# Experts of the second layer: a fixed TensorE order, gate and up side by side, mix in row groups

## The chip, the cores and the metric

The kernel runs on one core of one Trainium2 chip. The metric is the device time of one execution in microseconds (us), the median of several runs. The core has five engines with queues of their own: TensorE (PE; its weight loads are shown as PEld), VectorE (DVE), ScalarE (ACT), GpSimd (POOL) and SyncE (SP), which issues most of the DMAs.

## What is computed

A model of two layers runs over 256 tokens and 256 context tokens, 1024 wide. Each layer is a mixer (a recurrent scan, a neighbourhood attention and a sliding-window attention) and a mixture of 16 experts, of which each token takes two. In the second layer only the 256 tokens are left. The change touches that layer's experts:

```python
def moe(h, w_router, router_bias, w_gate, w_up, w_down):
    ...
    y = jnp.zeros_like(h)
    for e in range(N_EXPERTS):
        he = jax.nn.silu(h @ w_gate[e]) * (h @ w_up[e])
        y = y + gates[:, e:e + 1] * (he @ w_down[e])
    return y

# in reference(), last layer
f = moe(h2.reshape(-1, d), w_router, router_bias, w_gate[l], w_up[l], w_down[l]).reshape(x.shape)
x = layer_norm(alpha * x + g2 * f, ln2_g[l], ln2_b[l])
```

`gates` is zero but for two experts of a token. An expert's weights are three matrices, 1024 x 512 twice and 512 x 1024, 6 MiB in float32.

## The kernel before

**Capacities.** The kernel sorts the experts by how many tokens chose them and gives the place in that order a fixed capacity. In the second layer these are 64 for places 0 to 2, 128 for place 3, 64 for places 4 to 10 and 32 for places 11 to 15. A path for tokens that don't fit (`rerun`) follows under a condition and isn't taken here.

**One expert in the second layer** (`experts1`), with the tiles' names as the profile shows them:

1. The six pieces of its weights, 1 MiB each (`wload`), come in order over SP's queue into a ring of 16 pieces of SBUF. A piece's load waits until the matmuls that read the piece's last content have ended.
2. `hgather`: 48 small bfloat16 matmuls with a one-hot matrix (`oh`) put the expert's tokens, transposed, into PSUM (tile `hgt`); ScalarE copies them to region C.
3. `half`, for gate and then for up: `contract` multiplies the tokens (stationary) with the weights (moving, 512 columns) in float32, eight steps of k; each is two MATMUL instructions in the trace. A stationary matrix of 64 columns fills half of the array's columns, so two steps of k stand side by side, in two column groups (four for capacity 32). Their sums lie in different partitions of one PSUM bank (tile `gu`).
4. `whole` adds these row groups up: one ScalarE copy and one VectorE addition for two groups, one copy and three additions for four. `glu` applies SiLU on ScalarE and multiplies gate by up, on POOL for all but the last expert.
5. `htrans`: four transposes (tile `hT`), a ScalarE copy to region A.
6. `down`: `contract` again, into two banks (tile `dn`), one for each half of the 1024 columns, with two or four row groups each.
7. `weigh`: ScalarE scales both banks by the gate value into a rounded float32r part, and VectorE writes the remainder; VectorE also makes the matrix (`st`) that sends rows back to tokens. `slot` supplies the token numbers and gate values for that, by two small matmuls.
8. `mix`: eight float32r matmuls, 128 rows by 512 columns, add the expert's rows into four PSUM banks that stay for the whole layer (tile `acc`): this also adds the row groups of `down` up.

**Order.** The instructions are written in a software pipeline: the gate half of expert i, the transposes of i - 1, the slot of i + 1, the mix of i - 2, the up half of i, the gather of i + 1, down of i - 1. A scheduler may move an instruction ahead of others on its engine where no dependence forbids it.

**Staging region.** Elsewhere in the kernel float32 weights are split into two float32r parts in region S (16 K elements a partition, K = 256), which `split` fills in turn. In the second layer's experts S holds the scaled rows of `weigh`.

**After the experts** come the residual, a layer norm and the output.

Of the kernel before, what the change touches and what calls it, by code (L numbers as in the profile page):

```python
# [67 lines left out]
REGIONS = {"A": 16 * K, "B": 8 * K, "C": 8 * K, "S": 16 * K}  # L68
# [103 lines left out]

class _Builder:
    def __init__(self, tc, ap, out, dbg=None, caps=CAPS):
        self.tc, self.nc, self.ap, self.out, self.dbg, self.caps = tc, tc.nc, ap, out, dbg or {}, caps
# [5 lines left out]
    def run(self):  # L181
        tc = self.tc
        with ExitStack() as ctx:
# [19 lines left out]
            with tc.If(cnt > 0):  # L203
                self.general, self.native, self.map = True, False, BANKS
                self.lastw = self.hold = self.lastg = None
# [55 lines left out]
    def split(self, raw, dst=None):  # L261
        if dst:
            hi, lo = dst
        else:
            n = raw.shape[1]
            u = n // 256
            m = sum(t.shape[1] for t in self.sring) // 512
            if self.nsp % m + u > m:
                self.nsp += m - self.nsp % m
            o = (self.nsp % m) * 512  # L270
            self.nsp += u
            r = self.sring[0]
            if o >= r.shape[1]:
                o, r = o - r.shape[1], self.sring[1]
# [239 lines left out]
    def mixer(self, l):  # L514
        self.tokens_in()
        self.ring_of("S")
# [694 lines left out]
    def finish(self, l, T, rows):  # L1211
# [108 lines left out]
        self.ring_of("S")  # L1320
# [255 lines left out]
    def hsplit(self, i, cap, put):  # L1576
        nc = self.nc
        if self.single(cap):
            if not self.native:
                self.ring_of("S")  # L1580
# [23 lines left out]
    def contract(self, pbs, h, w):  # L1604
# [3 lines left out]
        if len(h) == 1:  # L1608
            m = P // cap
            for g in range(0, nk, m):  # L1610
                for j, pb in enumerate(pbs):
                    for i in range(m):
                        o = ((g + i) * n + j) * 512
                        t = slice(i * cap, (i + 1) * cap)
                        nc.tensor.matmul(pb[t], h[0][:, g + i], w[o // PIECE][:, o % PIECE:o % PIECE + 512],  # L1615
# [10 lines left out]
        return [pb[:cap] for pb in pbs]  # L1626

# [25 lines left out]
    def htrans(self, i, a, cap, pb=None):  # L1653
# [13 lines left out]
        for k in range(4):  # L1667
            nc.tensor.transpose(pb[:, k * cap:(k + 1) * cap], av[:, k, :], self.ident[:cap, :cap])  # L1668
# [26 lines left out]
    def wload(self, l, e, names):  # L1695
        out = []
        for n in names:
            for i in range(2):
                t = self.ring[self.nr % len(self.ring)]
                self.nr += 1  # L1700
                eng = self.nc.sync
                if e < self.fix:
                    src = self.ap[n][l * NE + e]
                else:
                    src = self.ap[n][bass.ds(self.expert(l, e - self.fix), 1)].rearrange("o p c -> p (o c)")
                self.lastw = eng.dma_start(t, src[:, i * PIECE:(i + 1) * PIECE])
                out.append(t)
        return out
# [7 lines left out]
    def start(self, l):  # L1716
# [12 lines left out]
        self.ring_of("S") if l else self.ring_of("C", "S")  # L1729
# [140 lines left out]
    def hgather(self, i, cap):  # L1870
# [3 lines left out]
        def put(o, k):  # L1874
            for tb, v in enumerate(oh):
                for j in range(3):
                    nc.tensor.matmul(o, self.hp[tb][j][:, k, :], v[:, :cap], start=tb + j == 0, stop=3 * tb + j == n - 1)  # L1877
# [3 lines left out]
    def slot(self, i, pi):  # L1881
        nc, oh = self.nc, self.oh
        M = oh[0].shape[1]
        for tb, v in enumerate(oh):
            nc.tensor.matmul(pi[:M, :5], v, self.meta[:, tb, i, :], start=tb == 0, stop=tb == 1)
# [5 lines left out]
    def weigh(self, i, pys, T):  # L1891
        nc = self.nc
        M = pys[0].shape[0]
        o = i % 2 * 2 * D
        y = [self.region("S")[:M, o + j * D:o + (j + 1) * D] for j in range(2)]
# [9 lines left out]
        def mix():  # L1905
            for tb in range(2):
                for n in range(2):
                    for j in range(2):
                        nc.tensor.matmul(self.pf[tb][n], oT[tb], y[j][:, n * 512:(n + 1) * 512],  # L1909
# [4 lines left out]
    def experts1(self, T):  # L1914
# [10 lines left out]
        load = lambda i, *names: self.wload(l, i, ["w_" + n for n in names])  # L1925
        gu = {0: load(0, "gate", "up")}
# [5 lines left out]
        a, h4, dn, ps = {}, {}, {}, {}  # L1932
        mix = None

        def down(i):
            return self.weigh(i, self.down(h4[i], dn[i]), T)

        def turn(i):
            pb = self.bank("hT")
            h4[i] = self.htrans(i, a[i], caps[i], pb)  # L1940
            return pb[:, 256:] if caps[i] <= 64 else self.bank("sl")

        self.slot(0, self.bank("sl"))
        for i in range(NE):
# [162 lines left out]
```

## Time and profile before

| | us |
|---|---|
| median of 3 runs | 1202.23 (1201.42 to 1206.09) |
| profiled execution | 1204.09 |
| its span | 1202.3 |
| busy in the span: PE / DVE / ACT / POOL | 1087.1 / 781.9 / 555.7 / 147.4 |
| granted TensorE clock, mean | 0.955 |
| read from HBM | 316.27 MB |

The span is the time from the first to the last instruction that the profiler recorded. A line of the kernel that is a helper's stands for all its callers, so tiles' names say more than lines. PEclk, or the granted clock, is the share of 2.4 GHz that TensorE got; it has two levels, 2.4 and 1.2 GHz, and a value between them is a mean over a stretch. "<-" behind an idle time names the engine and tile that ended it.

### The profile page before, as it was taken

Reading aid. Unit: us, or ns where it says so; the run is one execution under the profiler, and the core shown is the slowest. Engines: PE = TensorE matmul, PEld = TensorE weight load, DVE = VectorE, ACT = ScalarE, POOL = GpSimd, SP = SyncE. Lnnn points to the kernel's source line nnn. Section 1 sums busy time; section 2 is a strip of 40 time slices with the busy share of each in tenths; the row PEclk is TensorE's granted clock in tenths of the full one; section 3 lists DMA queues with packets and bytes.
Section 4 is the critical chain, followed back from the end, with each engine's and each line's share of the span. In section 5 each row is a group of like instructions: output and inputs, shape, how many; then the busy total and the mean of one; then the engine's idle time right before and its main releaser. Section 6 shows DMA issues by size and latency. Waiting matters only on the chain.

```text
span 1202.3 us, 18417 instructions
## 1 busy us (share of the span) xinstructions
PE 1087.1 (90%) x6813; PEld 700.1 (58%) x6813; DVE 781.9 (65%) x1742; ACT 555.7 (46%) x910; POOL 147.4 (12%) x151
## 2 busy tenths in 40 slices
PE   5999999999995999999999689999995899999872
PEld 3766766755684777676443587677664444444331
DVE  3466779757789998888324874787867622333545
ACT  2364335446643876787433644524465222222232
POOL 0000111100001243444210000010000000000000
PEclk9999999999996999999999899999896999999996
DMA  9756665634467999899999723565085699999951
GB/s 378 277 218 255 239 251 213 244 123 145 163 226 245 334 359 335 310 388 393 372 410 414 291 86 136 183 227 191 15 323 206 275 390 342 394 422 421 420 224 39
DMA packets 55044, 326.88 MB, mean 272 GB/s; under 512 B 9435, under 2 KB 9691, under 8 KB 19616
## 3 DMA queue, kind: packets, MB, share of 16 engines
q1 hardware_dynamic: 43920, 275.34, 59.5%
q0 software_dynamic: 9152, 50.10, 11.1%
q8 instruction: 56, 0.92, 0.3%
q10 hardware_dynamic: 1872, 0.16, 0.1%
q14 instruction: 44, 0.36, 0.1%
HBM read 316.27 MB, written 13.09 MB: 274 GB/s over the span
## 4 chain that ended last, share of the span: by engine, by line
PE 71%; DVE 15%; DMA 6%; ACT 5%; issue 2%; POOL 1%; SPq 0%; POOLq 0%; ACTq 0%; DVEq 0%
PE gu L1615 12%; PE proj L414 11%; PE gu L1624 7%; PE dn L1615 6%; PE op L709 4%; PE dn L1624 4%; PE first L414 3%; DMA G<-in_w_ada_dram 3%; PE acc L1909 2%; PE ada L393 2%; PE hgt L1877 2%; PE pt L1122 2%; PE S L1099 2%; PE py L1129 2%; PE hT L1668 1%
## 5 line engine op out<-in xcount | busy, mean ns | idle before, releaser
L276 ACT CAST S<-G 128x1024 fp32r<-128x1024 f32 (+2 forms) x162 | 156.9, 975 | 164.0 <-PE proj L414 108.2
L286 DVE TENSOR_TENSOR S<-G,S 128x1024 fp32r<-128x1024 f32 (+2 forms) x144 | 166.8, 1168 | 79.2 <-ACT S L276 76.9
L414 PE MATMUL proj<-A,S 128*128 128x512 f32 (+1 forms) x672 | 184.2, 355 | 2.8 <-ACT S L276 1.4
L1615 PE MATMUL gu<-G,C 128*64 128x512 f32 (+2 forms) x672 | 145.4, 602 | 1.4 <-ACT C L1597 1.4
L414 PEld LDWEIGHTS proj<-A,S 128*128 128x128 f32 x672 | 118.5, 192 | 28.9 <-issue 8.4
L1615 PEld LDWEIGHTS gu<-G,C 128*64 128x64 f32 (+2 forms) x672 | 43.4, 133 | 81.0 <-issue 76.1
L1624 PE MATMUL gu<-S,A 128*128 128x512 f32 (+3 forms) x300 | 76.6, 397 | 3.5 <-POOL S L284 2.2
L1624 PEld LDWEIGHTS gu<-S,A 128*128 128x128 f32 (+3 forms) x300 | 52.0, 177 | 20.3 <-POOL S L284 3.1
L414 PE MATMUL proj<-B,S 128*128 128x512 f32 (+1 forms) x168 | 60.2, 359 | 1.2 <-DVE B L1286 1.2
L1637 DVE TENSOR_TENSOR vt<-vt,gu 64x512 f32<-64x512 f32 (+1 forms) x31 | 21.1, 680 | 61.5 <-ACT vt L1634 61.2
L709 PE MATMUL op<-S,A 128*128 128x512 f32 x176 | 60.6, 407 | 0.0
L414 PE MATMUL proj<-C,S 128*128 128x512 f32 (+1 forms) x168 | 58.2, 348 | 0.0
L1647 POOL TENSOR_TENSOR tmp<-tmp,vt 64x512 f32<-64x512 f32 (+1 forms) x14 | 17.9, 1277 | 300.5 <-DVE vt L1637 286.5
L386 POOL DMA_DIRECT2D G<-in_w_ada_dram x40 | 22.3, 558 | 256.9 <-PE ada L393 172.2
L1637 DVE TENSOR_TENSOR tmp<-tmp,gu 64x512 f32<-64x512 f32 (+1 forms) x31 | 21.1, 680 | 50.1 <-ACT tmp L1634 49.7
L1615 PE MATMUL dn<-G,A 128*64 128x512 f32 (+2 forms) x240 | 53.3, 630 | 0.0
L1624 PE MATMUL dn<-S,B 128*128 128x512 f32 (+3 forms) x192 | 52.2, 406 | 0.4
L1624 PE MATMUL gu<-C,A 128*128 128x512 f32 (+3 forms) x180 | 48.5, 400 | 1.8 <-DVE C L286 1.8
L1567 POOL DMA_INDIRECT G<-h2d,idx x16 | 22.3, 1392 | 218.5 <-DVE oh L1551 140.5
L276 ACT CAST C<-G 128x1024 fp32r<-128x1024 f32 x38 | 39.8, 1047 | 12.3 <-PE gu L1624 7.7
L1901 DVE SCALAR_TENSOR_TENSOR S<-dn,slot,S 128x512 fp32r<-128x512 f32 x32 | 23.6, 749 | 31.9 <-ACT S L1900 30.6
L1111 ACT ACTIVATE G<-G,nm 128x512 f32<-128x512 f32 x48 | 34.5, 719 | 20.6 <-DVE nm L1109 10.2
(434 smaller groups left out, 2169.8 us busy)
## 6 DMA issues: line engine op xcount, KB each, us to landing
G<-in_w_gate_dram SPq DMA_DIRECT2D x62, 1024.0 KB, 7.9
G<-in_w_up_dram SPq DMA_DIRECT2D x62, 1024.0 KB, 8.0
G<-in_w_down_dram SPq DMA_DIRECT2D x62, 1024.0 KB, 9.5
G<-in_w_ada_dram POOLq DMA_DIRECT2D x40, 1024.0 KB, 6.7
G<-in_w_in_dram SPq DMA_DIRECT2D x22, 1024.0 KB, 8.7
G<-in_w_out_dram SPq DMA_DIRECT2D x12, 1024.0 KB, 6.3
G<-in_w_ada_dram SPq DMA_DIRECT2D x8, 1024.0 KB, 15.7
G<-vd SPq DMA_DIRECT2D x12, 512.0 KB, 4.6
```

What stands on the lines that cost most here:

```text
L276: self.lasts = [self.nc.scalar.copy(hi, raw)]
L286: self.lasts.append(sub(lo, raw, v))
L393: nc.tensor.matmul(pb[g:g + 32, i * 256:(i + 1) * 256], self.sT[:, kb, :], w[i][:, kb * 256:(kb + 1) * 256], start=kb < 4, stop=kb >= 4, t ...
L414: self.nc.tensor.matmul(pb[:, t], a[:, c], m, start=first and n == 0 and i == 0, stop=last and n == len(kbs) - 1 and i == 2)
L709: nc.tensor.matmul(pbs[tb][h], a, w[j][h], start=n == 0 and i == 0, stop=n == KB - 1 and i == 2)
L1099: nc.tensor.matmul(pb, qT[r, qb * P:(qb + 1) * P], kT[r, :], start=True, stop=True)
L1111: nc.scalar.activation(Pt, Pt, AF.Exp, scale=-1.0, bias=m, accum_out=ls[:, i:i + 1])
L1122: nc.tensor.transpose(pt[:, k * P:(k + 1) * P], Ps[i][:, k * P:(k + 1) * P], self.ident)
L1129: nc.tensor.matmul(py[r, :NX], V(hh, k), PT[hh][:, k, :], start=k == 0, stop=k == 3)
L1615: nc.tensor.matmul(pb[t], h[0][:, g + i], w[o // PIECE][:, o % PIECE:o % PIECE + 512], start=g == 0, stop=g + m == nk, tile_position=(0, i ...
L1624: nc.tensor.matmul(pbs[j][:cap], h[a][:, k], ws[b][:, c], start=k == 0 and q == 0, stop=k == nk - 1 and q == 2)
L1637: self.nc.vector.tensor_add(out, out, pb[i * cap:(i + 1) * cap])
```

## The change

- Gate and up of an expert of capacity 64 or 32 are computed together: half of the array's column groups hold gate, half up, for the same k (`tiles`). With capacity 64 there is nothing left to add up; with 32 there are two row groups for each, one copy and one addition (`fused`). SiLU reads PSUM, and the product is VectorE's. The pieces are loaded in the order gate, up, gate, up.
- `down` of these experts puts the two halves of the 1024 columns side by side in one bank (`outs`), so `weigh` scales one bank, and `mix` uses 64-row matmuls: the upper and lower half of the rows, each in a row group of the array and each into a bank of its own.
- TensorE's instructions of this stage are chained: each must follow the one written before it (`_Chained`). They are written in a new order: gather of i + 1, mix of i - 1, slot of i + 1, transposes of i, first gate-and-up half of i + 1, down of i, second half of i + 1.
- Region S becomes two tiles, S and T, of 8 K each. T is the 17th piece of the ring in the second layer's experts.
- The expert of capacity 128 keeps `contract`, in the new order.

```diff
-REGIONS = {"A": 16 * K, "B": 8 * K, "C": 8 * K, "S": 16 * K}
+REGIONS = {"A": 16 * K, "B": 8 * K, "C": 8 * K, "S": 8 * K, "T": 8 * K}
...
+class _Chained:
...
+    def _then(self, i):
+        if self.last is not None:
+            self.b.behind(i, self.last)
+        self.last = i
+        return i
...
+    def twin(self, cap):
+        return self.native and 2 * cap <= P
+
+    def tiles(self, pb, h, src, ks):
+        nk, cap = h[0].shape[1:]
+        q = P // cap // 2
+        for g in range(ks.start, ks.stop, q):
+            for j in range(2):
+                for i in range(q):
+                    o = (j * q + i) * cap
+                    self.pe.matmul(pb[o:o + cap], h[0][:, g + i], src(g + i, j), start=g == 0, stop=g + q == nk,
+                                   tile_position=(0, o))
+        return pb
+
+    def outs(self, h, w):
+        part = lambda k, n: w[k // 2][:, (2 * (k % 2) + n) * 512:(2 * (k % 2) + n + 1) * 512]
+        return self.tiles(self.bank("dn"), h, part, range(4))
+
+    def fused(self, pb, cap):
+        nc = self.nc
+        a = self.st("tmp", 512)[:cap]
+        g, u = (pb[j * P // 2:j * P // 2 + cap] for j in range(2))
+        if 4 * cap <= P:
+            for j, v in enumerate((a, self.st("vt", 512)[:cap])):
+                o = j * P // 2
+                nc.scalar.copy(v, pb[o + cap:o + 2 * cap])
+                nc.vector.tensor_add(v, v, pb[o:o + cap])
+                g, u = (v, u) if j == 0 else (g, v)
+        nc.scalar.activation(a, g, AF.Silu)
+        nc.vector.tensor_mul(a, a, u)
+        return a
...
         def mix():
+            if len(pys) == 1:
+                for tb in range(2):
+                    for j in range(2):
+                        for n in range(2):
+                            p = slice(n * P // 2, (n + 1) * P // 2)
+                            self.pe.matmul(self.pf[tb][n], oT[tb][p], y[j][p], start=i + j == 0,
+                                           stop=i == NE - 1 and j == 1, tile_position=(n * P // 2, 0))
+                return
...
+        self.ring.insert(-1, self.region("T", F32))
+        names = [("w_gate", 0), ("w_up", 0), ("w_gate", 1), ("w_up", 1)]
...
+        self.pe = _Chained(self)
...
         for i in range(NE):
-            ps[i] = [self.half(h[i], gu[i][0:2])]
...
-            pb = turn(i - 1) if i else self.bank("sl")
...
+            a = self.fused(ps[i], caps[i]) if self.twin(caps[i]) else self.glu(ps[i], caps[i])
             if i < N:
-                self.slot(i + 1, pb)
+                gu[i + 1] = [gload(i + 1, 0)]
+            dn[i] = self.wload(l, i, ["w_down"])
+            if i < N:
+                gu[i + 1].append(gload(i + 1, 1))
+                h[i + 1] = self.hgather(i + 1, caps[i + 1])
             if mix:
                 mix()
-            ps[i].append(self.half(h[i], gu[i][2:4]))
-            a[i] = self.glu(ps[i], caps[i], eng=nc.gpsimd if i < N else None)
...
+                self.slot(i + 1, self.bank("sl"))
...
+            h4 = self.htrans(i, a, caps[i])
             if i < N:
-                h[i + 1] = self.hgather(i + 1, caps[i + 1])
-            if i:
-                mix = down(i - 1)
...
+                gate(i + 1, 0)
+            if i == N:
+                break
+            mix = self.weigh(i, [self.outs(h4, dn[i])] if self.twin(caps[i]) else self.down(h4, dn[i]), T)
+            gate(i + 1, 1)
```

TensorE's queue before, in the middle of the experts of capacity 64, from one gather to the next (a MATMUL row of gu, dn, acc or hT counts matmuls of the program; "oh" is the one-hot matrix, "st" the matrix of the mix):

```order
L1615 MATMUL dn<-G,A 64x512 x8
L1615 MATMUL gu<-G,C 64x512 x8
L1668 MATMUL hT<-con,tmp 128x64 x4
L1909 MATMUL acc<-S,st_8397 128x512 x4
L1885 LDWEIGHTS oh
L1885 MATMUL hT<-meta,oh 128x5
...
L1909 MATMUL acc<-S,st_8398 128x512 x4
L1615 MATMUL gu<-G,C 64x512 x8
```

The same place now, again from one gather to the next:

```order
L184 MATMUL acc<-S,st_8405 128x512 x4
L184 MATMUL acc<-S,st_8406 128x512 x4
L184 LDWEIGHTS oh
L184 MATMUL sl<-meta,oh 128x5
...
L187 MATMUL hT<-con,tmp 128x64 x4
L184 MATMUL gu<-G,C 64x512 x8
L184 MATMUL dn<-G,A 64x512 x8
L184 MATMUL gu<-G,C 64x512 x8
```

The mix and the transposes moved ahead of both gate-and-up halves, directly behind the gather, and down of the same expert moved between the halves of the next one; a step that stood between two halves of one expert is now between two experts.

ScalarE's queue before, over one expert of capacity 32 (tmp is the gate's row sum and then SiLU, vt the row sum of up, S the scaled rows, C the gathered tokens, A the transposed ones):

```order
L1597 COPY A<-hT 128x128
L1634 COPY tmp<-gu 32x512
L1643 ACTIVATE tmp<-tmp 32x512
L1597 COPY C<-hgt 128x256
L1634 COPY vt<-gu 32x512
L1900 ACTIVATE S<-dn,slot 128x512 x2
```

ScalarE's queue now, over one expert of capacity 32:

```order
L1670 COPY tmp<-gu 32x512
L1614 COPY C<-hgt 128x256
L1670 COPY vt<-gu 32x512
L1673 ACTIVATE tmp<-tmp 32x512
L1614 COPY A<-hT 128x128
L1950 ACTIVATE S<-dn,slot 128x512
```

Both copies of row sums now stand ahead of SiLU, with the copy of the gathered tokens between them, and one scaled copy is left of two. VectorE's additions on gu go from six to two for such an expert and from two to none for one of capacity 64.

## Rows read from the trace of the kernel before

**Rows 1.** Stretches: busy us (x instructions) of each engine, PEclk, DMA share, GB/s.
```profile
1030.00:1040.00 10.00, 10.00 (x50) 4.23 (x48) 3.94 (x10) 3.15 (x6) 0.70 (x1) 1.00 0.98 365
1043.00:1108.00 65.00, 65.00 (x511) 29.05 (x510) 23.49 (x48) 18.45 (x32) 6.35 (x5) 1.00 1.01 422
1108.00:1183.00 75.00, 60.96 (x536) 25.99 (x528) 37.00 (x75) 21.59 (x40) 5.09 (x4) 0.93 0.68 281
1170.00:1180.00 10.00, 7.41 (x28) 2.94 (x28) 4.72 (x8) 1.67 (x4) 0.00 (x0) 0.66 0.01 2
```
**Rows 2.** Chain of waits, one expert of capacity 64: start us, us, what.
```profile
1042.95 1.51 PE hgt L1877 x48
...
1051.47 0.62 PE hT L1668 x4
1052.10 1.13 PE acc L1909 x4
...
1053.27 1.03 PE acc L1909 x4
1054.31 3.58 PE gu L1615 x16
1057.89 1.51 PE hgt L1877 x48
```
**Rows 3.** Timeline of PE in the second mixer: start, us, engine, line, tile, shape.
```profile
853.22 0.71 PE L981 MATMUL lev<-G 64*128 64x128 f32 x8
...
854.75 1.04 PE L1122 MATMUL pt<-con,G 128*128 128x128 f32 x8
```
**Rows 4.** Chain of waits, first gate of expert 1 and of expert 11.
```profile
947.70 3.65 PE gu L1615 x16
...
1107.60 1.00 PE gu L1615 x8
```
**Rows 5.** Chain of waits, the experts of capacity 32.
```profile
1139.73 0.59 ACT tmp L1634
...
1142.51 1.37 PE hgt L1877 x48
...
1151.11 1.90 PE gu L1615 x16
...
1155.86 1.37 PE hgt L1877 x48
```
**Rows 6.** Groups by form, 934 to 1184 us: line, engine, tile, shape, count, busy, mean ns.
```profile
L1901 DVE SCALAR_TENSOR_TENSOR S<-dn,slot,S 128x512 fp32r<-128x512 f32 x32 | 23.6, 749 | 31.9 <-ACT S L1900 30.6
L1900 ACT ACTIVATE S<-dn,slot 128x512 fp32r<-128x512 f32 x32 | 21.5, 687 | 38.3 <-PE dn L1615 38.2
...
L1637 DVE TENSOR_TENSOR tmp<-tmp,gu 32x512 f32<-32x512 f32 x15 | 10.2, 682 | 8.4 <-ACT tmp L1634 8.0
...
L1903 DVE TENSOR_SCALAR st<-Sd,slot 128x128 fp32r<-128x128 f32 x32 | 9.0, 283 | 17.2 <-PE acc L1909 9.3 <-PE hT L1885 7.3
...
L1643 ACT ACTIVATE tmp<-tmp 32x512 f32<-32x512 f32 x5 | 3.1, 629 | 11.3 <-DVE tmp L1637 11.3
```
**Rows 7.** Timeline of ACT, the experts of capacity 32.
```profile
1143.97 0.37 ACT L1597 COPY C<-hgt 128x256 f32<-128x256 f32 x1 [0.85 <-PE hgt L1877]
```
**Rows 8.** Chain of waits, the last expert and the start of the final norm.
```profile
1174.53 2.00 PE acc L1909 x4
1176.53 3.54 PE dn L1615 x16
...
1182.42 1.29 DVE G L1982 x2
```
**Rows 9.** Line of the weight loads, from 930 us: count, durations, first and last start; landing.
```profile
L1706 SPq EVENT_SEMAPHORE  x81: 17/17/17, 940.0 to 1141.0; - x81
...
L1706 SPq DMA_DIRECT2D G<-in_w_down_dram x27: 328/333/338, 941.7 to 1144.9; - x27
...
DMA to landing us min/median/max: 5.1/9.2/13.8
```

More of the change, by code (lines that the diff above doesn't have):

```diff
@@ L1693, in apart, with wload @@
         self.scat.append(st)
-    def wload(self, l, e, names):
+    def wload(self, l, e, names, parts=None):
         out = []
[L1697 to L1707, printed above, removed]
+        for n, i in parts or [(n, i) for n in names for i in range(2)]:
+            t = self.ring[self.nr % len(self.ring)]
+            self.nr += 1
+            if e < self.fix:
+                src = self.ap[n][l * NE + e]
+            else:
+                src = self.ap[n][bass.ds(self.expert(l, e - self.fix), 1)].rearrange("o p c -> p (o c)")
+            self.lastw = self.nc.sync.dma_start(t, src[:, i * PIECE:(i + 1) * PIECE])
+            out.append(t)
         return out
@@ L1924, in experts1, with gload @@
         self.ti, self.gs = slot[:, 0], slot[:, 1]
-        load = lambda i, *names: self.wload(l, i, ["w_" + n for n in names])
-        gu = {0: load(0, "gate", "up")}
+        self.ring.insert(-1, self.region("T", F32))
+        names = [("w_gate", 0), ("w_up", 0), ("w_gate", 1), ("w_up", 1)]
+        def gload(i, j):
+            p = names[2 * j:2 * j + 2] if self.twin(caps[i]) else [(names[j][0], k) for k in range(2)]
+            return self.wload(l, i, None, p)
+        gu = {0: [gload(0, 0), gload(0, 1)]}
         h = {0: self.hgather(0, caps[0])}
@@ L1931, in experts1, with gate @@
             nc.gpsimd.tensor_scalar_add(self.iota[:, i * P:(i + 1) * P], self.con[:, C_IOTA:C_IOTA + P], float(i * P))
-        a, h4, dn, ps = {}, {}, {}, {}
+        self.pe = _Chained(self)
+        dn, ps = {}, {}
         mix = None
[L1935 to L1941, printed above, removed]
+        def gate(i, j):
+            if not self.twin(caps[i]):
+                ps.setdefault(i, []).append(self.half(h[i], gu[i][j]))
+            elif j:
+                ps[i] = self.tiles(ps[i], h[i], lambda k, n: gu[i][k // 4][n][:, k % 4 * 512:(k % 4 + 1) * 512], range(4, 8))
+            else:
+                ps[i] = self.tiles(self.bank("gu"), h[i], lambda k, n: gu[i][0][n][:, k * 512:(k + 1) * 512], range(4))
@@ L1968, in experts1 @@
             self.qload(l2[j], ap["lnr"][4 * l + 2 + j:4 * l + 3 + j, :].to_broadcast([P, D]))
-        mix()
-        last = down(N)
+        last = self.weigh(N, [self.outs(h4, dn[N])], T)
         self.behind(nc.scalar.activation(self.st("sg", 1), self.epl, AF.Sqrt), self.weighed)
```

54 lines of the change are left out of this document (32 added, 22 removed).

## The prediction, made before the changed kernel was run

> **What bounds the kernel now.** I read the table of stretches first, then the chain of waits inside each stretch, then single groups by form, then the weight loads. The second layer's experts run from 934 us to 1183 us, and they fall into two stages [rows 1]. From 1043 to 1108 us, the stage of the experts of capacity 64, TensorE is busy 65.00 of 65 us at full clock, while the DMA engines move 422 GB/s at a share of 1.01: two limits that touch. From 1108 to 1183 us, the five experts of capacity 32, TensorE is busy 60.96 of 75 us and the DMA falls to 281 GB/s: there neither is the limit, and the chain shows what is. One period of the first stage, from one gather (hgt) to the next, is 1042.95 to 1057.89 us = 14.94 us [rows 2]; all of it is TensorE, and 1.13 + 1.03 = 2.16 us of it are the eight matmuls of the mix (acc). One period of the second stage is 1142.51 to 1155.86 us = 13.35 us [rows 5], and in it the chain leaves TensorE: a ScalarE copy [rows 5], then three VectorE additions one behind another (15 for five experts, 0.68 us each [rows 6]), before the next gather starts.
>
> **The mix in row groups.** Before, eight 128-row matmuls of 512 columns, one after another. Now each is 64 rows deep, and two that stand next to each other use different row groups and different banks. The kernel has such pairs already: lev, 64*128, takes 0.71 us for 8, and pt, 128*128 with the same 128 columns, 1.04 us for 8 [rows 3]. Without the 0.27 us or so that the last one takes in each, that is 0.44 against 0.77 us, a factor of 0.57. Bounds for the mix: half, 1.08 us, if pairs run fully beside each other; 2.16 us if they don't. By the lev row 1.2 us; I take that, a saving of 0.96 us.
>
> **The stage of capacity 64.** Apart from the mix each expert issues as many matmuls of the same shape as before: gate and up were two 64-column groups with different k, now they are two groups with different weights; the down projection likewise. So I count from the measured chain. From the gate of expert 1 to that of expert 11 it runs 947.70 to 1107.60 us [rows 4]. In the new order the transposes and the mix come ahead of the gate, so one transpose group (0.62 us [rows 2]) and one mix (1.2 us) more lie in front of expert 11's gate; eight small mixes in the stretch save 8 x 0.96 = 7.7 us (expert 3, capacity 128, keeps the old form). Expert 11's gate starts at 1107.6 + 0.6 + 1.2 - 7.7 = 1101.7 us. Does TensorE wait? Before the transposes it needs SiLU and product: about 0.63 + 0.68 + 0.15 us of hand-overs = 1.5 us [rows 6], which lie beside the gather and the mix, 1.51 + 1.2 us. The copies of row sums, the POOL product and half of the scaled copies go away here, but all of it was hidden behind a TensorE that never waits, so I cost it at nothing. If the cover were gone it would cost 1.5 us per expert at most.
>
> **The stage of capacity 32.** Here the removed work counts. The two row sums took one copy and three additions each; now one and one. The new chain from the end of an expert's second gate-and-up half, with the durations of [rows 6] and [rows 7] and 0.05 us per hand-over: copy to 0.68; ScalarE then has the copy of the gathered tokens in its queue, which waits for the gather (1.37 us [rows 5]) and takes 0.37, to 1.82; the second copy to 2.43; the second addition to 3.16; a one-hot row (st) on VectorE, 0.28, to 3.45; the product, 0.68, to 4.13. So the transposes start at 4.2 us, of which gather and mix cover 2.6: TensorE stalls 1.6 us. Then 0.62 us of transposes, and gate-and-up half, down, gate-and-up half, 16 instructions each, at 1.90 [rows 5]: a period of 10.5 us against 13.35. Bounds: TensorE alone, 1.37 + 1.2 + 0.62 + 5.7 = 8.9 us, and the old 13.35.
>
> From expert 11's gate on: 1.90 + 3.58 (down of expert 10, 16 instructions like the gu of [rows 2]) + 1.90 = 7.4 us, to 1109.1; four periods of 10.5 us, to 1151.1. The last expert, counted from there: two copies, additions, SiLU and product to 2.8, transposes and their copy (0.37 as in [rows 7]) to 3.95, down 1.9 to 5.85, scaled copy 0.69 and VectorE's remainder 0.75 [rows 6] to 7.4, two pairs of the mix to 7.9: 1159.0 us. There the final norm starts on VectorE; before it started at 1182.42 us [rows 8] and the span ended at 1202.3, 19.9 us later, and it is not changed. That gives 1178.9 us. One more term: between 1170 and 1180 us the granted clock is 0.66 on average [rows 1], that is, part of it at 1.2 instead of 2.4 GHz, and the last down takes 3.54 us and four acc 2.00 [rows 8] where 1.90 and 1.13 are usual, 2.5 us in all. TensorE idled before it; in the new tail it idles less long, so I take 1.0 us of 0 to 2.5. Span: 1179.9 us.
>
> **The weight loads.** They could become the bound. Before, 81 loads of 1 MiB were left when TensorE started on the experts, each behind one wait on SP, the first wait at 940.0 us, the last load issued at 1144.9 [rows 9] and, by the median, landing 9.2 us later, at 1154. At 422 GB/s a load takes 1048.6 / 422 = 2.49 us, 81 take 201.3: some 12 us of gaps. Now the added ring piece is loaded ahead, so 80 are left, 199 us; the first two now come free together, at about 941.4 us, as one group of matmuls reads both. With the old gaps the last lands at 941.4 + 199 + 12 = 1152.5 us, and the last half of the last down needs it at 1151.1 + 3.95 + 0.95 = 1156.0. So 3.5 us of slack, and the ring piece is worth nothing by itself. Behind the last landing come half a down, the scaled copy and its remainder, two pairs of the mix, the norm and the clock's term: 0.95 + 1.44 + 0.5 + 19.9 + 1.0 = 24 us. Without gaps the loads set a floor of 1140.5 + 24 = 1165 us for the span. Making two tiles of one staging region (S and T) moves a few instructions of the first layer's mixer past one another and adds none; I cost it at nothing.
>
> Sum: the span falls from 1202.3 to 1179.9 us: 6 us by expert 11's gate, 16 us behind it. The profiled execution took 1204.09 us with 1.8 us around the span; the median of the three runs, 1202.23, lies at the span itself, so I forecast 1180 us.
>
> **Rivals.** *The mix doesn't pair*: each stays at 2.16 us. For it: acc uses another number format than lev and four times the columns, so the rows show a relative only. Against: both have the geometry of lev. Nine more on the path at 0.96 us (in the stage of capacity 32 they hide in the stall): 1189 us. *The small experts don't speed up*: the fixed order lets TensorE draw nothing ahead into a stall, where the old order put a gate half between; the period stays 13.35 us. Four times 2.85 us: 1191 us. For it: ScalarE's copy of the gathered tokens stands between the two copies. *The loads become the bound*: from 1030 to 1040 us they moved only 365 GB/s at a share of 0.98 [rows 1]. If that is what they can do beside this TensorE, 80 loads take 230 us, the last lands at 1173, and 24 us later the span ends: 1197 us, no measurable change. Against: 65 us at 422, and the low window is one in which single loads wait for a piece to come free.
>
> The Trainium skill has a rule that would make this the outcome: "DMA: Bandwidth & Descriptors", Specifications, gives a limit of about 358 GB/s of HBM per core. By it 80 loads take about 234 us, as an estimate, and the span stays at about 1201 us. The trace disagrees: 422 GB/s over 65 us.
>
> *Slower*: in the fixed order the transposes of every expert of capacity 64 wait for SiLU and product. It decides once that wait is over 2.2 us in each of the ten, that is, when the chain reaches 4.9 us instead of 1.5; and an idle TensorE then also falls to half its clock, which in [rows 1] cost 3.4 us of 10. At 2.2 + 3.4 us for ten experts: 1180 + 56 = 1236 us. Against: VectorE and ScalarE lose work there. *The change does nothing*: the order is fixed, but each step waits as long as before, 1202 us.
>
> **How the numbers follow.** Forecast (1174 to 1186) 0.56; better than that, towards the floor, 0.05; no pairing 0.15; slow small experts 0.11; bound by loads 0.06; nothing 0.02; slower 0.05. About 0.5%, 6 us, is what a measurement can tell. Faster: 0.56 + 0.05 + 0.15 + 0.11 = 0.87. Within: 0.06 + 0.02 = 0.08. Slower: 0.05. The range runs from 1170, halfway between the loads' floor, 1165, and what the old gaps make of the shortest period, 1152.5 + 24 = 1176, to 1192, which takes in the first two rivals.
>
> **What would show it.** Right: acc in groups of eight at about 1.2 us; a gather-to-gather period near 14.0 us in the middle; expert 11's gate near 1102; a period near 10.5 us behind it, with TensorE waiting for VectorE's product ahead of hT; the last weight landing near 1152; the first DVE of the final norm near 1159. Wrong: acc at 2.2 us; idle of TensorE put down to a DMA; idle ahead of hT in the middle stage; or a lower granted clock between 950 and 1100 us.

## The result, and the profile after

The changed kernel takes 1185.66 us (median of four runs, 1183.43 to 1188.44) against 1204.13 for the kernel before in the same comparison: a ratio of 0.9846, 95% interval 0.9821 to 0.9871. The forecast was 1180, its range 1170 to 1192. The profiled execution is the longest of the four, 1188.44 us, with a span of 1186.5 us and a mean granted clock of 0.947.

Stretches of the changed kernel, with the columns of [rows 1]. From 1043 to 1108 us TensorE is as full as before, and VectorE needs 13.50 us instead of 23.49. The next line runs to the end of the experts; there the DMA engines were at 0.68 before and are at 0.87 now.

```profile
1043.00:1108.00 65.00, 65.00 (x538) 29.24 (x538) 13.50 (x45) 10.99 (x20) 0.00 (x0) 1.00 1.01 421
1108.00:1170.00 62.00, 49.82 (x520) 21.07 (x512) 21.84 (x56) 16.88 (x32) 0.00 (x0) 0.88 0.87 360
```

The chain of waits over one expert of capacity 64 (start us, us, what), to be held against [rows 2]: the mix is one group of 1.13 us, where two groups, 1.13 and 1.03 us, stood before (x6 in its row: the chain names six of the eight matmuls). The period is 1035.03 to 1048.87 us = 13.84 us instead of 14.94, and all of it is TensorE.

```profile
1035.03 1.51 PE hgt L184 x48
1036.53 1.13 PE acc L184 x6
...
1037.80 0.62 PE hT L187 x4
1038.41 3.58 PE gu L184 x16
1042.00 3.43 PE dn L184 x16
1045.43 3.43 PE gu L184 x16
1048.87 1.51 PE hgt L184 x48
```

The chain over one expert of capacity 32 answers to [rows 5]: 1114.70 to 1124.64 us = 9.94 us instead of 13.35. Here TensorE waits from about 1117.3 us, when gather, mix and slot are done, to 1118.72: the copy of the gathered tokens (C) stands between ScalarE's two row-sum copies, as forecast. The next period is 9.95 us long, but the third, 1134.59 to 1145.87 us, takes 11.28: there the clock fell, and a gate half took 3.16 us instead of 1.85.

```profile
1114.70 1.31 PE hgt L184 x48
...
1116.09 0.37 ACT C L1614
...
1116.48 0.59 ACT vt L1670
...
1118.72 0.64 PE hT L187 x4
...
1124.64 1.31 PE hgt L184 x48
...
1139.28 3.16 PE gu L184 x16
```

What the forecast did not have is at the head. The timeline of TensorE (start, us, engine, line, operation, tiles, count, idle before it and what ended it): `slot` of expert 0 now stands between the halves of its gate and up, and waits 2.95 us for VectorE's `meta`; the second half then takes 5.18 us instead of 3.65, and expert 0's transposes wait another 1.10 us for VectorE's product. In [rows 4] expert 1's gate came at 947.70, 13.33 us after the first gather (934.37 us); here 956.08 - 937.46 = 18.62 us pass.

```profile
937.46 2.72 PE L1924 MATMUL hgt<-oh,A 128*128 128x64 bf16 x48 [0.70 <-DVE oh L1912]
940.91 3.65 PE L184 MATMUL gu<-G,C 128*64 128x512 f32 x16 [0.73 <-ACT C L1614]
947.51 0.19 PE L184 MATMUL sl<-meta,oh 128*128 128x5 bf16 x2 [2.95 <-DVE meta L1514]
947.64 5.18 PE L184 MATMUL gu<-G,C 128*64 128x512 f32 x16
...
955.46 0.69 PE L187 MATMUL hT<-con,tmp 64*128 64x64 f32 x4 [1.10 <-DVE tmp L1674]
956.08 3.65 PE L184 MATMUL gu<-G,C 128*64 128x512 f32 x16
```

The same place before:

```profile
934.37 2.72 PE L1877 MATMUL hgt<-oh,A 128*128 128x64 bf16 x48 [0.70 <-DVE oh L1865]
...
947.70 3.65 PE L1615 MATMUL gu<-G,C 128*64 128x512 f32 x16 [0.68 <-ACT C L1597]
```

The chain at the end, beside [rows 8]: the last down still runs at half the clock, 3.69 us where 1.72 is usual here. Ahead of it the second row-sum copy (vt) starts only when VectorE's first addition (tmp) has ended.

```profile
1154.10 1.79 PE gu L184 x16
...
1156.52 0.69 DVE tmp L1671
1157.23 0.59 ACT vt L1670
...
1160.52 3.69 PE dn L184 x16
...
1166.66 0.75 DVE G L2051 x2
```

The weight loads, as in [rows 9]: the last is issued at 1138.9 instead of 1144.9 us, but now it takes 19.8 us from issue to landing. SP now also waits for the landing of an earlier load before it issues the next one, ten times and 16.9 us in all; in the kernel before it waits for no landing from 940 us on.

```profile
L1753 SPq DMA_DIRECT2D G<-in_w_down_dram x25: 332/333/338, 945.7 to 1138.9; - x25
...
DMA to landing us min/median/max: 5.1/10.9/19.8
```

### The profile page after: what moved, and what is told of

It reads as the page before. It is cut to its first block, busy times and chain, and to the rows that moved or that the text cites. A ratio compares the mean times of both kernels' runs of the same rounds, so it can differ in the third digit from the quotient of the medians.

```text
span 1186.5 us, 18295 instructions
## 1 busy us (share of the span) xinstructions
PE 1071.6 (90%) x6813; PEld 694.7 (59%) x6813; DVE 742.3 (63%) x1701; ACT 533.1 (45%) x875; POOL 128.1 (11%) x137
## 4 chain that ended last, share of the span: by engine, by line
PE 71%; DVE 14%; ACT 4%; DMA 4%; issue 4%; POOL 1%; SPq 0%; ACTq 0%; DVEq 0%; POOLq 0%
PE proj L431 12%; PE gu L184 9%; PE gu L1641 6%; PE dn L184 4%; PE dn L1641 4%; PE op L726 4%; PE gu L1632 4%; DMA G<-in_w_ada_dram 3%; PE first L431 3%; PE ada L410 2%; PE pt L1139 2%; PE hgt L184 2%; PE dn L1632 2%; PE S L1116 2%; PE py L1146 1%
## 5 line engine op out<-in xcount | busy, mean ns | idle before, releaser
L293 ACT CAST S<-G 128x1024 fp32r<-128x1024 f32 (+2 forms) x83 | 79.3, 958 | 82.0 <-PE proj L431 54.3
L293 ACT CAST T<-G 128x1024 fp32r<-128x1024 f32 (+2 forms) x79 | 78.1, 994 | 84.5 <-PE proj L431 57.0
L303 DVE TENSOR_TENSOR S<-G,S 128x1024 fp32r<-128x1024 f32 (+2 forms) x75 | 85.8, 1147 | 44.4 <-ACT S L293 42.6
L303 DVE TENSOR_TENSOR T<-G,T 128x1024 fp32r<-128x1024 f32 (+2 forms) x69 | 82.4, 1198 | 39.7 <-ACT T L293 39.2
L431 PE MATMUL proj<-A,T 128*128 128x512 f32 (+1 forms) x336 | 99.7, 371 | 1.5 <-ACT T L293 1.0
L431 PE MATMUL proj<-A,S 128*128 128x256 f32 (+1 forms) x336 | 91.4, 351 | 1.4 <-DVE S L303 0.9
L431 PEld LDWEIGHTS proj<-A,T 128*128 128x128 f32 x336 | 62.0, 197 | 17.4 <-issue 5.4
L431 PEld LDWEIGHTS proj<-A,S 128*128 128x128 f32 x336 | 60.6, 198 | 11.9 <-issue 3.1
L1641 PE MATMUL gu<-T,A 128*128 128x512 f32 (+3 forms) x174 | 46.9, 399 | 3.3 <-POOL T L301 2.2
L1128 ACT ACTIVATE G<-G,nm 128x512 f32<-128x512 f32 x48 | 34.4, 718 | 21.1 <-DVE nm L1126 10.8
L1632 PE MATMUL gu<-G,C 128*64 128x512 f32 x192 | 43.0, 595 | 0.0
```

What stands on the lines that cost most here:

```text
L293: self.lasts = [self.nc.scalar.copy(hi, raw)]
L303: self.lasts.append(sub(lo, raw, v))
L431: self.nc.tensor.matmul(pb[:, t], a[:, c], m, start=first and n == 0 and i == 0, stop=last and n == len(kbs) - 1 and i == 2)
L1128: nc.scalar.activation(Pt, Pt, AF.Exp, scale=-1.0, bias=m, accum_out=ls[:, i:i + 1])
L1632: self.pe.matmul(pb[t], h[0][:, g + i], w[o // PIECE][:, o % PIECE:o % PIECE + 512], start=g == 0, stop=g + m == nk, tile_position=(0, i * ...
L1641: nc.tensor.matmul(pbs[j][:cap], h[a][:, k], ws[b][:, c], start=k == 0 and q == 0, stop=k == nk - 1 and q == 2)
```

## Experiments

Diffs are against the changed kernel where nothing else is said. Two numbers of each run count: the time, and, since the part ahead of the experts varies from run to run (the first gather lies between 930.69 and 940.93 us in twelve executions whose code ahead of it is the same), the *stage*, from the first gather to the first VectorE instruction of the final norm in the profiled execution. Each ratio is to the kernel before in its own comparison; its median there lay between 1203.62 and 1204.63 us.

| kernel | median us | ratio to before (95%) | stage us |
|---|---|---|---|
| before | 1204.63 | | 248.1 |
| changed, profile above | 1185.66 | 0.9846 (0.9821 to 0.9871) | 229.2 |
| changed, again | 1184.63 | 0.9829 (0.9800 to 0.9859) | 225.9 |
| slot later | 1180.96 | 0.9808 (0.9778 to 0.9837) | 225.7 |
| ring of 16 | 1187.12 | 0.9855 (0.9827 to 0.9883) | 232.5 |
| order only | 1194.02 | 0.9908 (0.9877 to 0.9938) | 240.0 |
| mix reordered | 1185.30 | 0.9830 (0.9804 to 0.9856) | 229.4 |
| new form for 32 only | 1191.59 | 0.9889 (0.9864 to 0.9914) | 239.3 |
| no fixed order | 1210.68 | 1.0054 (1.0037 to 1.0071) | 256.4 |
| copies first | 1180.44 | 0.9808 (0.9780 to 0.9836) | 226.0 |
| one row group | 1202.54 (one run) | | 239.8 |
| column groups last | 1215.23 (one run) | | 252.8 |
| waits filled | 1178.63 | 0.9793 (0.9764 to 0.9821) | 224.3 |

**The changed kernel again.**

> The changed kernel as it is, beside the other runs on one chip. Theory and rivals alike: 1183 to 1188 us. If the 3.1 us by which its second layer's experts started later than before (first gather at 937.46 against 934.37 us) belong to that one execution, the first gather lies near 934 to 936 us in this one; if the change of the staging region in the first layer costs them, it lies near 937.5 again.

1184.63 us; first gather at 936.05 us, between the two. As it scatters over 10 us in the twelve executions, on both sides of the 934.37 us before, I put the 3.1 us down to chance. The stage is 3.3 us shorter than in the first profile, for two reasons. The head takes 953.14 - 936.05 = 17.09 us instead of 18.62: `meta` is ready 10.05 us after the first gather in both, but here the lower clock fell into the first half (5.92 us), so that `slot` waits 0.69 us only and the second half is back at 3.65:

```profile
939.50 5.92 PE L184 MATMUL gu<-G,C 128*64 128x512 f32 x16 [0.73 <-ACT C L1614]
946.10 0.19 PE L184 MATMUL sl<-meta,oh 128*128 128x5 bf16 x2 [0.69 <-DVE meta L1514]
```

And the last down takes 1.97 us instead of 3.69.

**Slot later.**

```diff
         gate(0, 0)
         self.hold = None
+        gate(0, 1)
         self.slot(0, self.bank("sl"))
         self.onehot(l, 1)
-        gate(0, 1)
```

> Expert 0's slot matmuls come behind both halves of its gate-and-up, not between them. Theory: the wait of 2.95 us for VectorE's meta was a new wait of the fixed order and pulled the next half to half clock (5.11 instead of 3.4 to 3.6 us), so both go: expert 1's gate starts about 4.5 us earlier after the first gather and the time falls by 3 to 5 us, to about 1181. Rival: VectorE is late as a whole there, so TensorE only waits at the next place (ahead of expert 0's transposes, 1.1 us before, then about 4 us): no change, 1185 us.

In this execution both halves run through at full clock, and `slot` finds its `meta` ready; expert 1's gate starts 946.71 - 933.42 = 13.29 us after the first gather, as in the kernel before:

```profile
936.87 7.09 PE L184 MATMUL gu<-G,C 128*64 128x512 f32 x32 [0.73 <-ACT C L1614]
943.89 0.20 PE L184 MATMUL sl<-meta,oh 128*128 128x5 bf16 x2
...
946.71 3.65 PE L184 MATMUL gu<-G,C 128*64 128x512 f32 x16
```

So the wait was one of place, not of a late VectorE. The lower clock at the head is another matter: in the profiles of the last two kernels below, which have `slot` in this place too, the same 32 instructions take 8.97 and 9.11 us and the head 15.17 and 15.31 us. It comes there without a wait of `slot`. The median falls by 3.7 us, as expected, but the intervals overlap; the stage of this execution is no shorter, since three stretches at half clock fell into its experts of capacity 32 and its last down.

**Ring of 16.** The line that inserts T into the ring is left out.

> The weights' ring keeps its old number of pieces, 16. Theory: no measurable change (within 2 us of the changed kernel), the last load lands about 2.5 us later and still ahead of the last down projection. Rival, the loads bound the changed kernel: each period of the experts shows TensorE waiting for a DMA, and the time rises by 2.5 us or more, to 1188 to 1195.

By its time, 2.5 us above the changed kernel with overlapping intervals, it can't be settled; the stage is 3.3 us longer than in the changed kernel's first profile. The timeline of the last expert's gate and up shows a wait that no profile of the changed kernel has:

```profile
1150.19 1.05 PE L184 MATMUL gu<-G,C 128*32 128x512 f32 x4 [0.48 <-DMA G<-in_w_gate_dram]
1152.62 0.62 PE L184 MATMUL gu<-B,C 128*32 128x512 f32 x2 [1.38 <-DMA B<-in_w_up_dram]
```

The two waits are 1.86 us, and as they cut the half in pieces it ends, where the mix starts, 1154.46 - 1149.71 = 4.75 us after the down ahead of it, where 1.79 us are usual. The added piece is worth about 3.0 us in this execution: little, but not nothing.

**Order only.**

```diff
     def twin(self, cap):
-        return self.native and 2 * cap <= P
+        return False
-        last = self.weigh(N, [self.outs(h4, dn[N])], T)
+        last = self.weigh(N, [self.outs(h4, dn[N])] if self.twin(caps[N]) else self.down(h4, dn[N]), T)
```

> The fixed order and the ring alone: small experts keep the old form of gate, up, down, row sums and mix. Theory: in the stage of capacity 64 each mix takes 2.0 to 2.2 us again (+0.9 to 1.0 us for about nine experts); in the stage of capacity 32 the chain behind the last gate-and-up half has three additions instead of one again (+1.4 us) and the mix of 2.1 us covers 0.9 us of it, period 11.2 to 11.6 instead of 9.94 us; the last expert about 2 us later. Sum: 15 to 17 us above the changed kernel, about 1200 to 1202 us, so the order by itself is worth next to nothing. Rival, the order is the gain: within 4 us of the changed kernel, 1185 to 1189 us. Rival, the old row sums need the freedom to draw a gate half into the stall: period 13.4 us and more, 1207 us or more.

Between the theories: 1194.02 us, half of the gain. The parts were near what was expected, the mix 1.94 to 1.95 us and the period of capacity 32 11.07 us (1128.11 to 1139.18, expected 11.2 to 11.6), the third addition of the second row sum in its chain:

```profile
1128.11 0.63 PE hT L187 x4
...
1137.54 0.69 DVE vt L1686
...
1139.18 0.64 PE hT L187 x4
```

The profiled execution, at 1201.38 us the longest of six (1189.36 to 1201.38), is where the sum had put it; the median is not. That execution has a mean clock of 0.945, the other five 0.950 to 0.958. Its stage is 10.8 us longer than in the changed kernel's first profile and 14.1 longer than in its second, so the 15 to 17 us were too many by this measure too; which term was too large is open.

**New form for capacity 32 only.**

```diff
-        return self.native and 2 * cap <= P
+        return self.native and 4 * cap <= P
```

(and the line of the last expert as above)

> Only the experts of capacity 32 have the new form; those of capacity 64 keep theirs, in the fixed order. Theory: in the stage of capacity 64 TensorE never waits, so the copies and additions that come back there cost nothing and only the mix counts: 1.94 instead of 1.12 us for nine mixes, 7.4 us: about 1192, and the period of capacity 32 stays near 9.95 us. Rival: side-by-side gate and up is worth something of its own at capacity 64 (TensorE waits ahead of the transposes without it): 1196 us or more.

1191.59 us: the first theory, though closer than the runs can tell. The chain shows the mix at 1.94 us and a period of 14.57 us instead of 13.84, all of it TensorE:

```profile
1046.91 1.51 PE hgt L184 x48
1048.42 1.94 PE acc L184 x8
...
1061.48 1.51 PE hgt L184 x48
```

From expert 1's to expert 11's gate 157.8 us pass (951.27 to 1109.09 us), where the changed kernel takes 151.3: 6.5 us, nine periods at 0.73. The rest of the stage's difference to the changed kernel's first profile, 10.1 us, is no part of the theory: 1.4 us at the head, where `slot` now waits 3.49 us and the half behind it takes 6.54, and 2.2 us behind expert 11's gate.

So of the mix's 2.16 us the order takes 0.2, by keeping the eight together, and the row groups 0.8; gate beside up is worth next to nothing at capacity 64, since the period's 0.73 us are no more than the mix's 0.81. In the kernel before, one mix stands together, at 1004.00 us, and it takes 1.97 us.

**Mix reordered.**

```diff
-                for tb in range(2):
-                    for j in range(2):
-                        for n in range(2):
+                for n in range(2):
+                    for tb in range(2):
+                        for j in range(2):
```

> The small mixes keep their eight 64-row matmuls, reordered so that neighbours use the same row group. Theory (the saving is two row groups beside each other): acc x8 at 1.9 to 2.1 us instead of 1.12; +0.8 to 0.95 us for each of the eight or nine small mixes in the stage of capacity 64, none in the stage of capacity 32, where TensorE waits 1.46 us behind the mix anyway: 6 to 8 us above the changed kernel, about 1191 to 1192. Rival (matmuls of 64 rows are cheaper by themselves, whatever stands next to them): acc stays near 1.1 us and the time near 1185.

No change: 1.14 us, 1185.30 us. The theory that the two row groups must alternate is wrong. The single records of the trace say how: the eight still start in pairs, the two of the first pair 13 to 14 ns apart (3 to 4 ns in the changed kernel), though written four and four.

```profile
1037.84 1.14 PE acc L184 x8
```

**One row group.**

```diff
-                            p = slice(n * P // 2, (n + 1) * P // 2)
+                            p = slice(0, P // 2)
-                                           stop=i == NE - 1 and j == 1, tile_position=(n * P // 2, 0))
+                                           stop=i == NE - 1 and j == 1, tile_position=(0, 0))
```

> The small mixes use rows 0 to 63 for both column halves, so that all eight matmuls stand in one row group (the other row group's product is left out, the first one stands in its place). Theory after the reordered mix, which took 1.14 us: the engine finds a partner in the other row group by itself, up to three matmuls further on; with no partner at all acc x8 takes 1.9 to 2.1 us. Rival: a matmul of 64 rows in this number format takes half as long as one of 128 rows, beside others or not; acc stays at 1.1 us.

With no partner at all the same eight matmuls take 2.06 us, starting 0.23 to 0.35 us after one another. A period is 1056.05 - 1041.29 = 14.76 us instead of 13.84. The one run took 1202.54 us, with the latest first gather of all:

```profile
1042.79 2.06 PE acc L184 x8
```

Two row groups are the gain, then, and a matmul finds its partner past three others of its own group. Whether the two need banks of their own was not tested. If matmuls only started in the order issued, the fifth, first of the other group, would start behind the fourth: 3 x 0.22 us later, and eight would take some 1.14 + 0.65 = 1.8 us (0.22 being an eighth of 2.06 less the 0.27 or so of the last).

The Trainium skill says in "TensorE: Matmul & The Clock Gate", Part 3, The mechanism, that weight loads are pulled ahead but matmuls start and end strictly in order. The 1.14 us, and the pairs in which the records start, disagree with that for starts.

**Column groups last.** The same for gate, up and down: all matmuls of one column group behind one another.

```diff
-        for g in range(ks.start, ks.stop, q):
-            for j in range(2):
-                for i in range(q):
+        for j in range(2):
+            for i in range(q):
+                for g in range(ks.start, ks.stop, q):
```

> Gate-and-up halves and down of the small experts issue the matmuls of one column group behind one another (for capacity 32 two, for capacity 64 four), instead of going round the groups. Theory (four column groups run beside each other only where four different ones stand next to each other; in the free order the pieces x2 and x10 of a half took 1.85 and 2.7 us): a half of capacity 32 takes 2.6 to 3.5 us instead of 1.72, a half of capacity 64 5 to 7 us instead of 3.43, period of capacity 64 18 us or more instead of 13.85. Rival: the engine finds partners by itself as in the reordered mix; 1.72 and 3.43 us stay.

Between theory and rival. At capacity 32, two in a row of each group, nothing is lost (transposes at 1145.10 and 1155.11 us, 10.01 us apart). At capacity 64, where four in a row are eight instructions in the trace, a period takes 15.83 us instead of 13.84, and part of each group runs beside that of the next step:

```profile
1036.57 0.62 PE hT L187 x4
1037.19 4.06 PE gu L184 x13
1041.25 0.06 PE dn L184
...
1052.40 0.62 PE hT L187 x4
```

Past three instructions of its own group one finds a partner without loss, past seven only in part.

**No fixed order.** `self.pe = _Chained(self)` is left out.

> The new forms and the ring without the fixed order. Built, its order in the stage of capacity 64 is the same, slot's matmuls of expert 0 come later, and in the stage of capacity 32 halves of gate-and-up and the mix stand between the product and the transposes. Theory: the fixed order itself gains nothing and costs the wait at its head (4 us); TensorE's waits of 1.46 us go too, but by then the weight loads are the limit (they ran at 420 GB/s to the end), so some of that comes back as waits for a DMA: 1179 to 1182 us. Rival, the fixed order is what makes the small experts fast: 1190 us or more, period of capacity 32 over 11 us. Rival, no limit by the loads: 4 + 5 x 1.46 = 11 us less, about 1174.

My theory falls: the new forms without the order are slower than the kernel before. The stage of capacity 64 is as good (13.84 us a period), but a period of capacity 32 takes 17.0 us on average (transposes at 1116.15, 1134.34, 1152.01, 1168.95 and 1184.09 us). Pieces from the chain of one, and below them two rows of other views, the wait at its end and the stretch's busy times and clock:

```profile
1116.84 1.85 PE gu L1655 x2
...
1120.08 2.71 PE gu L1655 x10
...
1127.59 0.98 PE gu L1655 x4
```

```profile
1134.34 0.69 PE L1717 MATMUL hT<-con,tmp 32*128 32x32 f32 x4 [3.50 <-DVE tmp L1674]
```

```profile
1116.00:1134.00 18.00, 13.83 (x110) 4.58 (x110) 3.96 (x12) 3.01 (x6) 0.00 (x0) 0.78 1.01 423
```

Three things add up. Gather and mix no longer stand between the last gate-and-up half and the transposes, so nothing covers the row sums and TensorE waits 3.50 us instead of 1.46. The halves are cut: 4 instructions take 0.98 us (at full clock) where 16 take 1.72 us in one piece, because column groups run beside each other only while their matmuls stand near, as the run before shows. And the clock is 0.78. How much each makes was not taken apart. The order is what makes the small experts fast.

**Copies first**, on top of slot later: SiLU and both row-sum copies ahead of the copy of the gathered tokens.

```diff
-        self.nc.scalar.copy(dst[0], src)
+        self.behind_silu(self.nc.scalar.copy(dst[0], src))
...
-        nc.scalar.activation(a, g, AF.Silu)
+        self.sil = (nc.scalar.activation(a, g, AF.Silu), None)[4 * cap > P]
...
+    def behind_silu(self, c):
+        if self.sil is not None:
+            self.behind(c, self.sil)
+            self.sil = None
```

> Expert 0's slot later as in the run before, and for capacity 32 ScalarE's copy of the gathered tokens behind both row-sum copies and SiLU, not between the two copies. Theory 1: the wait ahead of the transposes falls from 1.46 to about 0.4 us, period about 8.9 us, four times 1.0 us: about 1177 us against 1181 with slot alone. Theory 2, the weight loads are the limit now (in the kernel with slot alone the last ones landed within 1 to 3 us of their use): the wait ahead of the transposes falls, but TensorE waits as much for a DMA in the last two experts, no gain: 1180 to 1182 us. I hold theory 2.

No gain that can be told, 1180.44 us, and neither theory explains it: in the profile TensorE waits for no DMA. The order on ScalarE is the new one, but its second copy waits for VectorE's first addition, so the wait ahead of the transposes falls from 1.46 to 1.09 us only, and a period from 9.95 to 9.57 (transposes at 1119.35 and 1128.92 us; in the other two a half at the lower clock makes it 11.23 and 11.05):

```profile
1104.56 0.58 ACT L1670 COPY tmp<-gu 32x512 f32<-32x512 f32 x1 [1.16 <-PE gu L184]
1105.88 0.58 ACT L1670 COPY vt<-gu 32x512 f32<-32x512 f32 x1 [0.74 <-DVE tmp L1671]
...
1107.02 0.37 ACT L1614 COPY C<-hgt 128x256 f32<-128x256 f32 x1
```

The two instructions share no result, but both read the same PSUM bank. No run here takes the bank apart, so the cause stays open.

The Trainium skill, "PSUM — Partial Sum Buffer", section "PSUM bank collisions raise a hardware error", asks for semaphores between engines by bank and quadrant of 32 partitions, and calls by bank alone the simple version. Here the copy reads partitions 96 to 127 of the bank and the addition 0 to 31, so the wait of 0.74 us agrees with the simple version only.

**Waits filled**, on top of copies first.

```diff
+            self.warm((0, 4, 11)[(4 * caps[i] <= P) + (i == N)])
             h4 = self.htrans(i, a, caps[i])
...
+        self.warm(1)
         last = self.weigh(N, [self.outs(h4, dn[N])], T)
+        self.warm(3)
...
+    def warm(self, n):
+        if n:
+            pb, v = self.bank("hgt"), self.hp[0][0]
+            for _ in range(n):
+                self.pe.matmul(pb, v[:, 0, :], v[:, 0:4, :], start=True, stop=True)
```

> On top of the kernel with slot later and SiLU ahead of the gathered tokens' copy: TensorE gets matmuls whose result nobody reads where it waits: 4 of 128x512 in bf16 ahead of the transposes of experts 11 to 14, 11, 1 and 3 in the waits of the last expert. Theory: it is the idle time that brings the lower clock; the last down takes 1.72 instead of 3.69 us, its acc 0.55 to 0.9 us less, the single gate halves of 3.3 to 3.5 us fall to 1.85: 4 to 6 us less, about 1175 us. Rival: the lower clock comes without idle time, or the added matmuls run into what follows: no gain, 1180 us or more.

The granted clock is now 1.00 from 1095 to 1155 us, in copies first 0.90, no uncut gate half of capacity 32 computes for over 1.92 us, and the last down takes 1.97: idle time was what brought the clock down in this stage. At the head, where the idle time was not filled, the lower clock is still there (9.11 us, as told above). The stretch with the waits filled:

```profile
1095.00:1155.00 60.00, 57.02 (x606) 25.06 (x610) 20.22 (x56) 17.30 (x34) 0.00 (x0) 1.00 0.96 398
```

But the gain is 1.8 us (median; 1.7 by the stage), less than the runs can tell, because the next limit shows at the last expert:

```profile
1142.66 1.05 PE L184 MATMUL gu<-G,C 128*32 128x512 f32 x4 [0.30 <-DMA G<-in_w_gate_dram]
1145.13 1.91 PE L184 MATMUL gu<-G,C 128*32 128x512 f32 x12 [1.43 <-DMA G<-in_w_up_dram]
```

TensorE waits 1.73 us for the loads, which run at 419 to 424 GB/s from 1095 to 1145 us, and with the half cut by these waits its end comes 1147.04 - 1142.36 = 4.68 us after the down ahead of it instead of 1.79: 2.9 us are lost to the loads. The chain that ended last is now made of loads: one issued at 1105.61 us lands 19.62 us later, only then, at 1125.34 us, another is issued, and when that has landed, 19.75 us later, the half goes on.

This is the fastest version, 1178.63 us (1177.14 to 1182.04); against the kernel before it is clear, against the changed kernel the intervals still touch.

## Why the prediction was right, and what it missed

The forecast's mechanism held in the main, and the time lies in the range. That it lies no further from 1180 is luck in part: 10.3 us that the sum did not have are set off by 3.7 us in which its parts were too slow. Point by point:

- *The mix in row groups*: 1.12 to 1.14 us against 1.2. Two row groups are needed for it (one row group 2.06 us), but not the alternation that the text named.
- *The stage of capacity 64*: TensorE never waits, and only the mix counts; shown by the new form for 32 alone (+7.0 us in the median, 7.4 expected). From expert 1's to expert 11's gate 151.3 us pass, where the sum has 1101.7 - 947.7 = 154.0 (with the 0.6 us of expert 0's transposes, which lie ahead of expert 1's gate now and so in the head below); 8 x 0.14 = 1.1 us is the shorter period, the rest was not taken apart.
- *The stage of capacity 32*: 9.94 us against 10.5, the wait ahead of the transposes 1.46 against 1.6, both from the chain that was written down. The mix's shorter time and faster gate halves (1.72 instead of 1.90) make the difference. The clock took some of it back in the third period (11.28 us). The 13.35 us before, on which the price of the second rival rests, was the shortest of three periods; the others took 14.27 and 14.30 us.
- *The loads*: forecast to land with 3.5 us of slack. The last is issued at 1138.9 and takes 19.8 us, so it lands near 1158.7; the second half of the last down, which reads it, starts near 1160.52 + 3.69 / 2 = 1162.4 us: 3.7 us. That this matches is luck: both lie over 6 us later than forecast (1152.5 and 1156.0). That the ring piece is worth nothing was not right: without it TensorE waits 1.9 us and loses 3.0, not ahead of down but ahead of the last half of gate and up, where the slack is smaller. (In the rival that is bound by loads, 941.4 + 230 is 1171.4, not 1173 us.)
- *The step that failed* is the one that asks "Does TensorE wait?" and finds no wait: it looked at the transposes, and not at the other instruction that the new order puts on the chain at its head, `slot` of expert 0. The fixed order makes a wait of 2.95 us there; behind it a stretch at half clock took 1.5 us more, and a second wait came ahead of expert 0's transposes, 1.10 us. The head cost 18.62 - 13.33 = 5.3 us that the sum has at 0, but for the 0.6 us named above. With slot later both waits are gone (13.29 us). The half clock is not shown to come from the wait: it fell into the head in profiles without it as well.
- *A term mis-sized* is the last expert, 7.9 us forecast (and 1.0 for the clock). From the end of its gate and up to the norm it took 1166.66 - 1155.89 = 10.8 us, as the last down and mix ran wholly at half clock; in the profile of the changed kernel run again, with the last down at 1.97 us, 8.7 us. The 0.8 us that are left there are an overlap that the sum had wrong: it runs the second row-sum copy beside the first addition, and the copy waits for that addition (1157.23 behind 1156.52 + 0.69 us).

Of the 6.6 us by which the span exceeds the forecast, 5.3 are the head, 10.8 - 7.9 - 1.0 = 1.9 the last expert, 3.1 the later start; the two stages give 2.7 and 0.9 us back, and the norm 0.1.

Where the gain comes from: fixed order and ring alone make 10.6 us (1204.63 to 1194.02), the new form for capacity 32 some 2.4 more (to 1191.59; the intervals overlap, so this part isn't clear), that for capacity 64 some 7.0 (to 1184.63). These don't add up freely: the new forms without the order lose 7.

## What to carry over

When an order is fixed, every instruction that stands on it becomes a place where the whole engine can wait, so walk the whole chain, its first round above all, and ask of each who supplies it. Matmuls that share the array by row or column groups are worth their price only while their partners stand near; check that neither a scheduler nor a late load cuts the sets. And where two limits touch, price the second before spending on the first: filling the waits brought the full clock and gained only 1.8 us in the median, since the loads were next.

## What was not expected of the hardware

- A matmul runs beside one of another row group even when three of its own group stand in between (1.14 us for eight, against 2.06 in one group), and with eight instructions of one column group in a row still partly (period 15.83 against 13.84 us).
- With the loads at their limit a load takes 19.8 us from issue to landing, eight times the 2.49 us that 1 MiB takes at 421 GB/s, so by estimate some eight are on the way. In that stretch SP issues the next load only when an earlier one has landed.
- One core drew 421 GB/s from 1043 to 1108 us, and from 1095 to 1155 us again. The Trainium skill, "HBM Reference", Specifications (TRN2), states about 425 GB/s for a core that streams alone; the traces agree, so the limit of 358 weighed in the prediction isn't one for this kernel.
